# A transposition through DRAM with runs of 512 bytes, whole-piece column scales, and one piece turned on TensorE

## The chip, the cores and the metric

The kernel runs on one core of one Trainium2 chip. The metric is the device time of one execution in microseconds, the median of three runs. Names of engines: PE is TensorE, DVE VectorE, ACT ScalarE, POOL GpSimd, SP the queue engine that issues most transfers.

## The reference

Two layers of a trunk on a sequence of 256 positions and a model width of 2048, all float32. One layer in short:

```python
h = rmsnorm(x, g_pre)
u = h @ w_in                       # latents, B's q k v z, C's q k v z, A's z, gate logits
o_a = latent attention             # q and k normalised and scaled by column gains
o_b = differential attention       # bq = rope(rmsnorm(b_q, b_g_q)), bk likewise, heads of 2 x 64
o_c = chunked band attention       # cq = rmsnorm(c_q, c_g_q), ck likewise, heads of 128
branches = (o_a * silu(a_z), o_b * silu(b_z), o_c * silu(c_z))
y = sum(gates[n] * (branches[n] @ w_branch[n]) for n in range(3))
x = x + y @ w_out
```

Every product with a weight matrix contracts over the feature axis, so whatever was computed with positions on the partitions (q, k, the gated branch outputs, y, and x for the next layer) has to be transposed before it is multiplied again.

## The kernel before

The 256 positions are two row tiles of 128. All weights are streamed from DRAM once, in units of 512 output columns (`matunit`, L138 to L166). A unit walks over its rows in chunks of 256: SP issues the DMA of a chunk of 512 KB (tile `..._r`, L153, four buffers), ACT rounds it to the matmul format (`..._h`, L154, three buffers), DVE subtracts to get the rest (`..._l`, L155, three buffers), and PE does 12 matmuls of 128x512 with them: data hi times weight hi (L163), times weight lo (L164), and data lo times weight hi (L165). A unit over 2048 rows has 8 such chunks.

In the B and C halves (`b0`, `b1`, `c0`, `c1`, four heads each) the units come in the order k, q, v, z, and then the scores (L311 and L317). k and q are normalised with positions on the partitions (`qk_natural`), then transposed by `bounce`, and `from_bounced` splits the transposed piece to hi and lo with the column gain applied as a scale of ACT's and DVE's operation: L174 and L175 for C, L186 and L187 for B's q (`split_stacked`, four operations of 64x512 on each engine), L195 and L196 for B's k (`split_twice`, eight on each).

`bounce` (L218) transposes a piece of 256x512 in this way: DVE turns blocks of 32x32 in place (L223, two operations), one DMA writes the piece to DRAM in runs of 2 KB (L225), and four DMAs read it back, one for each 32 partitions, in runs of 32 floats = 128 bytes (L229, a source of 32 x 32 x 32). All five go by SP's queue, in order with the weight chunks. There are 42 such pieces over both layers: the latent (2), k and q of B and C (16), gated outputs of A and C (8) and of B (4), y (8) and x for layer 1 (4). On PE the same can be done by `to_transposed` (L202): eight transposes of 128x128 into PSUM, from where ACT and DVE split to hi and lo; so far branch A uses it.

At a layer's end `gate_branch(2)` makes the last of y, four pieces of 512 columns (`n2j0` to `n2j3`; product `l1n2j3b_p`, gate and sum on DVE at L655 and L657 into `yacc`). Each piece is bounced (`l1n2j3yz`) and split (`l1n2j3y`, L171 and L172). The output projection (`l1o_p`) contracts over y: its first unit needs y0 to y3 in turn.

The order on each engine is set at build time by the tile framework's scheduler, from a timing model of its own. An engine works its instructions off strictly in that order.

## Time and profile before

| | us |
|---|---|
| median of 3 runs (lowest, highest) | 2031.13 (2028.79, 2031.28) |
| the profiled execution | 2029.23 |
| its span, first to last instruction | 2027.3 |

All durations below come from the profiled execution. PE is busy for 1985.4 us of the span, DVE for 1267.4, ACT for 1107.0; the clock that PE was granted is at its full level in nearly all of the 40 slices of the page. Of 293,325 DMA packets 187,328 are under 512 bytes. In a timeline, a row gives the start, the duration, the engine and the line, what is written from what, how many like it are drawn together (x2), and in square brackets how long the engine had been idle before and who released it. "SPq" is the issue of a transfer, not the transfer.

### The profile page before, as it was taken

The numbers are of one execution on the slowest core, as the hardware profiler recorded it, in microseconds if no ns is written. First come the engines' busy times: TensorE is split into PE (matmuls) and PEld (weight loads), VectorE is DVE, ScalarE is ACT, GpSimd is POOL, SyncE is SP. The second block draws the span as 40 slices with busy tenths as digits, with TensorE's granted clock in tenths as the row PEclk, the third lists the DMA queues.
The fourth block names the chain that finished last, engine by engine and source line by source line (L and its number), as shares of the span: only waits on it lengthen the run. The fifth ranks groups of instructions, "written<-read, shape, count | busy, mean of one in ns | idle before, by whom it ended". The sixth has DMA issues, their size and how long they took to land.

```text
span 2027.3 us, 25409 instructions
## 1 busy us (share of the span) xinstructions
PE 1985.4 (98%) x9112; PEld 1647.3 (81%) x9112; DVE 1267.4 (63%) x1750; ACT 1107.0 (55%) x1624; POOL 225.4 (11%) x357
## 2 busy tenths in 40 slices
PE   9999999999999999998999999999999999999989
PEld 7888778888888888887888887788888888888867
DVE  5778777545666555555657777775456665555544
ACT  6677667545555544443556766664456564444433
POOL 2313040001000000000023220400010100000000
PEclk9999999999999999999999999999999999999989
DMA  8765565666776656677886665756676676657774
GB/s 295 219 188 175 186 207 187 207 204 209 223 210 212 192 191 197 215 235 241 260 237 205 180 181 173 227 178 209 204 220 214 203 217 189 196 197 211 235 228 156
DMA packets 293325, 421.39 MB, mean 208 GB/s; under 512 B 187328, under 2 KB 191424, under 8 KB 292432
## 3 DMA queue, kind: packets, MB, share of 16 engines
q1 hardware_dynamic: 290992, 410.80, 65.4%
q0 software_dynamic: 1920, 8.46, 1.3%
q8 instruction: 71, 1.16, 0.2%
q14 instruction: 54, 0.44, 0.1%
q10 hardware_dynamic: 288, 0.52, 0.1%
HBM read 393.51 MB, written 26.21 MB: 207 GB/s over the span
## 4 chain that ended last, share of the span: by engine, by line
PE 77%; DMA 8%; ACT 4%; POOL 3%; DVE 3%; issue 3%; SPq 2%; ACTq 0%; POOLq 0%; DVEq 0%
PE l1g_p L164 4%; PE l1g_p L165 4%; PE l1g_p L163 4%; PE l0g_p L164 4%; PE l0g_p L165 4%; PE l0g_p L163 4%; SPq L229 2%; PE l1o_p L163 1%; PE l1o_p L165 1%; PE l1o_p L164 1%; PE l0o_p L164 1%; PE l0o_p L163 1%; PE l0o_p L165 1%; DMA l0cq_r<-w 1%; PE l1az_p L164 1%
## 5 line engine op out<-in xcount | busy, mean ns | idle before, releaser
L155 DVE TENSOR_TENSOR l1g_l<-l1g_r,l1g_h 128x1024 fp32r<-128x1024 f32 x96 | 117.3, 1222 | 94.4 <-ACT l1g_h L154 94.3
L155 DVE TENSOR_TENSOR l0g_l<-l0g_r,l0g_h 128x1024 fp32r<-128x1024 f32 x96 | 117.2, 1222 | 93.3 <-ACT l0g_h L154 93.2
L154 ACT CAST l0g_h<-l0g_r 128x1024 fp32r<-128x1024 f32 x96 | 101.1, 1053 | 130.0 <-PE l0g_p L165 79.8
L154 ACT CAST l1g_h<-l1g_r 128x1024 fp32r<-128x1024 f32 x96 | 101.1, 1054 | 127.8 <-PE l1g_p L165 78.1
L164 PE MATMUL l0g_p<-l0g_l,xh 128*128 128x512 f32 x384 | 149.8, 390 | 0.0
L165 PE MATMUL l0g_p<-l0g_h,xl 128*128 128x512 f32 x384 | 149.7, 390 | 0.0
L164 PE MATMUL l1g_p<-l1g_l,xh 128*128 128x512 f32 x384 | 149.7, 390 | 0.0
L165 PE MATMUL l1g_p<-l1g_h,xl 128*128 128x512 f32 x384 | 149.7, 390 | 0.0
L163 PE MATMUL l1g_p<-l1g_h,xh 128*128 128x512 f32 x384 | 136.0, 389 | 0.0
L163 PE MATMUL l0g_p<-l0g_h,xh 128*128 128x512 f32 x384 | 136.0, 390 | 0.0
L164 PEld LDWEIGHTS l0g_p<-l0g_l,xh 128*128 128x128 f32 x384 | 72.1, 188 | 15.3 <-DVE l0g_l L155 0.5
L164 PEld LDWEIGHTS l1g_p<-l1g_l,xh 128*128 128x128 f32 x384 | 72.1, 188 | 14.8
L165 PEld LDWEIGHTS l1g_p<-l1g_h,xl 128*128 128x128 f32 x384 | 72.1, 188 | 14.7
L165 PEld LDWEIGHTS l0g_p<-l0g_h,xl 128*128 128x128 f32 x384 | 72.1, 188 | 14.7
L163 PEld LDWEIGHTS l0g_p<-l0g_h,xh 128*128 128x128 f32 x384 | 72.1, 188 | 14.7
L163 PEld LDWEIGHTS l1g_p<-l1g_h,xh 128*128 128x128 f32 x384 | 72.0, 188 | 14.7
L155 DVE TENSOR_TENSOR l1o_l<-l1o_r,l1o_h 128x1024 fp32r<-128x1024 f32 x32 | 39.2, 1224 | 46.1 <-ACT l1o_h L154 46.1
L154 ACT CAST l1o_h<-l1o_r 128x1024 fp32r<-128x1024 f32 x32 | 33.7, 1054 | 58.5 <-PE l1o_p L165 45.6
L155 DVE TENSOR_TENSOR l0o_l<-l0o_r,l0o_h 128x1024 fp32r<-128x1024 f32 x32 | 38.8, 1219 | 29.5 <-ACT l0o_h L154 29.5
L154 ACT CAST l0o_h<-l0o_r 128x1024 fp32r<-128x1024 f32 x32 | 33.3, 1051 | 39.5 <-PE l0o_p L165 32.0
L703 POOL DMA_DIRECT2D xres<-x x1 | 0.8, 784 | 309.5 <-DVE l0n2j3yz L223 309.5
L703 POOL DMA_DIRECT2D xres<-xscr x1 | 0.8, 792 | 308.8 <-DVE l1n2j3yz L223 308.8
(1600 smaller groups left out, 5866.3 us busy)
## 6 DMA issues: line engine op xcount, KB each, us to landing
l0g_r<-w SPq DMA_DIRECT2D x96, 512.0 KB, 3.6
l1g_r<-w SPq DMA_DIRECT2D x96, 512.0 KB, 4.2
l0o_r<-w SPq DMA_DIRECT2D x32, 512.0 KB, 4.9
l1o_r<-w SPq DMA_DIRECT2D x32, 512.0 KB, 4.4
l0az_r<-w SPq DMA_DIRECT2D x16, 512.0 KB, 4.7
l1az_r<-w SPq DMA_DIRECT2D x16, 512.0 KB, 4.7
l0b0k_r<-w SPq DMA_DIRECT2D x8, 512.0 KB, 3.7
l0b0q_r<-w SPq DMA_DIRECT2D x8, 512.0 KB, 3.3
```

Source lines behind the costliest of these rows:

```text
L154: state["cast"] = nc.scalar.copy(wh[:, ks, :N], wr[:, ks, :N])
L155: nc.vector.tensor_tensor(out=wl[:, ks, :N], in0=wr[:, ks, :N], in1=wh[:, ks, :N].bitcast(F32), op=ALU.subtract)
L163: nc.tensor.matmul(ps[t][:, :N], h[:, ts], wh[:, k2, :N], start=first, stop=False)
L164: nc.tensor.matmul(ps[t][:, :N], h[:, ts], wl[:, k2, :N], start=False, stop=False)
L165: nc.tensor.matmul(ps[t][:, :N], lo[:, ts], wh[:, k2, :N], start=False, stop=last)
L229: nc.sync.dma_start(flat[32 * j:32 * j + 32].rearrange("p (b i c) -> p b i c", b=HH, c=32), sv[j])
L703: nc.gpsimd.dma_start(xres, x_src.rearrange("(t p) d -> p t d", p=P))
```

## The change

`bounce` no longer turns in place. The DVE transposes write to a tile of their own (`..._tu`, from the pool of the z tiles), with the 32-wide blocks in another sequence, so that in DRAM the four blocks that one partition reads back lie side by side: each of the four reads is now 32 x 8 x 128 floats, in runs of 512 bytes instead of 128, 256 runs instead of 1024. In SBUF the piece then stands with the four 128-column blocks interleaved in steps of 32 columns (`bounced` and `as_bounced` are views of that), so the operations that split it read and write in runs of 32 elements.

The gain is applied first, by one ACT operation of 128x1024 in place over the whole piece (`from_bounced`, L251 in the changed file), and the split follows as plain copies and subtractions over the whole piece: `split_twice` has 4 + 4 operations of 64x1024 instead of 8 + 8 of 64x512, `split_stacked` 2 + 2 instead of 4 + 4. There are 20 such gain operations (16 for k and q of B and C, 4 for B's gated output). The latent and x keep the gain inside the split, block by block.

The last piece of y in each layer (`j = 3`) is not bounced; `to_transposed` turns it on PE (transposes at L204 in the changed file). 40 pieces go through DRAM instead of 42.

```diff
-    def split_twice(d0, d1, l0, l1, src, gain):
+    def split_twice(d0, d1, l0, l1, src):
         a, b = slice(0, 64), slice(64, P)
         for hi, lo, d, dl in ((a, b, d0, l0), (b, a, d1, l1)):
             for o in (hi, lo):
-                nc.scalar.activation(d[o], src[hi], AF.Copy, scale=gain[hi])
-                nc.vector.scalar_tensor_tensor(out=dl[o], in0=src[hi], scalar=gain[hi],
-                                               in1=d[hi].bitcast(F32), op0=ALU.mult, op1=ALU.subtract)
+                nc.scalar.copy(d[o], src[hi])
+                nc.vector.tensor_tensor(out=dl[o], in0=src[hi], in1=d[hi].bitcast(F32), op=ALU.subtract)
...
     def bounce(src, name, dst=None):
+        turned = zp.tile([P, NT, 4, HH, 32], F32, tag="z", name=f"{name}_tu")
+        scr = dram.tile([NT, P, 4, 128], F32, name=f"{name}_scr")
+        for t in range(NT):
+            nc.vector.transpose(turned[:, t].rearrange("p j b c -> p b j c"), src[:, t, :])
+        nc.sync.dma_start(scr.rearrange("t p j f -> p t (j f)"), turned.rearrange("p t j b c -> p t (j b c)"))
         dst = src if dst is None else dst
-        for t in range(NT):
-            nc.vector.transpose(dst[:, t, :], src[:, t, :])
-        scr = dram.tile([SEQ, 512], F32, name=f"{name}_scr")
-        nc.sync.dma_start(scr.rearrange("(t p) f -> p t f", p=P), dst)
-        sv = scr.rearrange("(i r) (b j c) -> j r b i c", r=32, b=HH, j=4, c=32)
         flat = dst.rearrange("p t f -> p (t f)")
+        sv = scr.rearrange("t (i r) j f -> j r (t i) f", r=32)
         for j in range(4):
-            nc.sync.dma_start(flat[32 * j:32 * j + 32].rearrange("p (b i c) -> p b i c", b=HH, c=32), sv[j])
-        return flat.rearrange("p (b q) -> p b q", b=HH)
+            nc.sync.dma_start(flat[32 * j:32 * j + 32].rearrange("p (q f) -> p q f", f=128), sv[j])
+        return flat
+    def bounced(z, b=None):
+        v = z.rearrange("p (q b c) -> p q b c", b=HH, c=32)
+        return v if b is None else v[:, :, b, :]
...
     def from_bounced(z, dh, dl, gain, per_block=False, put=None):
+        if per_block:
+            for b in range(HH):
+                split(as_bounced(dh[:, b, :]), as_bounced(dl[:, b, :]), bounced(z, b), gain(b))
+            return
+        if gain is not None:
+            nc.scalar.activation(z, z, AF.Copy, scale=gain)
         if put is not None:
-            for b0 in (0, 2):
-                put(slice(b0, b0 + 2), z[:, b0:b0 + 2, :])
-        elif per_block:
-            for b in range(HH):
-                split(dh[:, b, :], dl[:, b, :], z[:, b, :], gain(b))
+            put(bounced(z), as_bounced)
         else:
-            split(dh, dl, z, gain)
+            split(as_bounced(dh), as_bounced(dl), bounced(z))
...
         def b_split(z, hf, name, gain=None):
...
-            split(bh[hf], bl[hf], z, gain)
+            from_bounced(z, bh[hf], bl[hf], gain)
...
-                from_bounced(bounce(nat, f"{n}{nm}T"), None, None, None, put=put)
+                from_bounced(bounce(nat, f"{n}{nm}T"), None, None, cg[:, 1:2] if i == 0 else cg[:, 4:5], put=put)
...
                     yh[j], yl[j] = yt[:, 0], yt[:, 1]
-                    yz = zp.tile([P, NT, 512], F32, tag="z", name=f"{nm}yz")
-                    from_bounced(bounce(yacc[:, :, js], f"{nm}yT", yz), yh[j], yl[j], None)
+                    if j < 3:
+                        yz = zp.tile([P, NT, 512], F32, tag="z", name=f"{nm}yz")
+                        from_bounced(bounce(yacc[:, :, js], f"{nm}yT", yz), yh[j], yl[j], None)
+                    else:
+                        to_transposed(lambda t: yacc[:, t, js], 4, yh[j], yl[j], None, f"{nm}yT")
```

The last y piece on PE, end of layer 0. `yacc` holds y, `l0o_p` is the output projection's first unit, `l0o_h` and `l0o_l` its weights. Before, the projection's matmuls on y3 follow those on y2 directly:

```order
L163 MATMUL l0o_p_7847<-l0o_h_7939,l0n2j2y 128x512
L164 MATMUL l0o_p_7847<-l0o_l_7940,l0n2j2y 128x512
L165 MATMUL l0o_p_7847<-l0o_h_7939,l0n2j2y 128x512
L163 MATMUL l0o_p_7846<-l0o_h_7957,l0n2j3y 128x512
L164 MATMUL l0o_p_7846<-l0o_l_7958,l0n2j3y 128x512
L163 MATMUL l0o_p_7847<-l0o_h_7957,l0n2j3y 128x512
```

Now the transposes stand among the matmuls of the projection, 26 matmuls behind the last one of the branch product, and the first matmul on y3 comes 46 rows behind the transposes:

```order
L165 MATMUL l0o_p_7854<-l0o_h_7874,l0n2j0y 128x512
L163 MATMUL l0o_p_7853<-l0o_h_7892,l0n2j1y 128x512
L163 MATMUL l0o_p_7854<-l0o_h_7892,l0n2j1y 128x512
L204 MATMUL l0n2j3yT_t_7835<-ident,yacc_3440 128x128
L204 MATMUL l0n2j3yT_t_7842<-ident,yacc_3440 128x128
L204 MATMUL l0n2j3yT_t_7835<-ident,yacc_3440 128x128 x3
L204 MATMUL l0n2j3yT_t_7842<-ident,yacc_3440 128x128 x3
L164 MATMUL l0o_p_7853<-l0o_l_7893,l0n2j1y 128x512
```

So PE has the turning of y3 in its own order, with work on y1 and y2 between it and the first use of the result.

ACT in half b0 of layer 0, around the split of q; `l0b0z_h` are weight casts, `l0a_low` and `l0a_pp` belong to branch A's attention. Before:

```order
L154 CAST l0b0z_h_2138<-l0b0z_r_2137 128x1024
L154 CAST l0b0z_h_2156<-l0b0z_r_2155 128x1024
L186 ACTIVATE l0b0q<-l0b0q_n,cgain 64x512 x2
L374 COPY l0a_low<-l0a_o 128x128
L171 CAST l0a_pp<-l0a_pt 128x384
L174 ACTIVATE l0b0v_v<-l0b0v_p_1984,rcol_326 128x512
L174 ACTIVATE l0b0v_v<-l0b0v_p_1985,rcol_326 128x512
L186 ACTIVATE l0b0q<-l0b0q_n,cgain 64x512 x2
L154 CAST l0b0z_h_2174<-l0b0z_r_2173 128x1024
```

Now:

```order
L154 CAST l0b0z_h_2151<-l0b0z_r_2150 128x1024
L388 COPY l0a_low<-l0a_o 128x128
L171 CAST l0a_pp<-l0a_pt 128x384
L154 CAST l0b0z_h_2169<-l0b0z_r_2168 128x1024
L251 ACTIVATE l0b0q_n<-l0b0q_n,cgain 128x1024
L183 CAST l0b0q<-l0b0q_n 64x8x4x32 x2
L174 ACTIVATE l0b0v_v<-l0b0v_p_1979,rcol_326 128x512
L174 ACTIVATE l0b0v_v<-l0b0v_p_1980,rcol_326 128x512
L154 CAST l0b0z_h_2187<-l0b0z_r_2186 128x1024
L388 COPY l0a_low<-l0a_o 128x128
```

The third cast of the z weights moved from behind the split of q to ahead of it.

ACT in half b1 of layer 0, around the split of k; `l0b1v_h` are the casts of the v unit's eight chunks. Before, six of them stand ahead of the split of k (the last two are shown) and two behind it:

```order
L154 CAST l0b1v_h_2990<-l0b1v_r_2989 128x1024
L154 CAST l0b1v_h_3008<-l0b1v_r_3007 128x1024
L195 ACTIVATE l0b1k_2696<-l0b1k_n,cgain 64x512 x4
L195 ACTIVATE l0b1k_2697<-l0b1k_n,cgain 64x512 x4
L154 CAST l0b1v_h_3026<-l0b1v_r_3025 128x1024
L154 CAST l0b1v_h_3044<-l0b1v_r_3043 128x1024
L154 CAST l0b1z_h_3069<-l0b1z_r_3068 128x1024
L186 ACTIVATE l0b1q<-l0b1q_n,cgain 64x512 x2
```

Now five stand ahead, and the sixth stands behind the gain and the four copies of k:

```order
L154 CAST l0b1v_h_2978<-l0b1v_r_2977 128x1024
L251 ACTIVATE l0b1k_n<-l0b1k_n,cgain 128x1024
L195 CAST l0b1k_2692<-l0b1k_n 64x8x4x32 x2
L195 CAST l0b1k_2693<-l0b1k_n 64x8x4x32 x2
L154 CAST l0b1v_h_2996<-l0b1v_r_2995 128x1024
L154 CAST l0b1v_h_3014<-l0b1v_r_3013 128x1024
L154 CAST l0b1v_h_3032<-l0b1v_r_3031 128x1024
L251 ACTIVATE l0b1q_n<-l0b1q_n,cgain 128x1024
L154 CAST l0b1z_h_3057<-l0b1z_r_3056 128x1024
```

The eight scaled operations became one gain and four copies, and one more weight cast has to wait for them; the gain of q (L251) also came ahead of the first cast of the z unit.

## Rows read from the trace of the kernel before

**Rows 1.** Page, part 1: busy us, share of the span, instructions.

```profile
PE 1985.4 (98%) x9112; PEld 1647.3 (81%) x9112; DVE 1267.4 (63%) x1750; ACT 1107.0 (55%) x1624; POOL 225.4 (11%) x357
```

**Rows 2.** PE's waits: line waited for, us in total, times, longest us.

```profile
PE l1o_p L163 <- ACT l1n2j3y L171: 8.0, 1, 8.0
PE l0o_p L163 <- ACT l0n2j3y L171: 6.1, 1, 6.1
PE l0b1v_p L163 <- ACT l0b1v_h L154: 2.4, 1, 2.4
PE l0c_s L311 <- ACT l0c1q L174: 1.6, 1, 1.6
PE l0b0z_p L163 <- ACT l0b0z_h L154: 1.6, 1, 1.6
PE l1b0z_p L163 <- ACT l1b0z_h L154: 1.5, 1, 1.5
PE l0b1z_p L163 <- ACT l0b1z_h L154: 1.2, 1, 1.2
PE l1b1z_p L163 <- ACT l1b1z_h L154: 1.2, 1, 1.2
```

**Rows 3.** PE timeline at both layer ends: start us, us, instruction, idle before it.

```profile
942.28 0.80 PE L163 MATMUL l0o_p<-l0o_h,l0n2j3y 128*128 128x512 f32 x1 [6.07 <-ACT l0n2j3y L171]
947.14 0.39 PE L165 MATMUL l0o_p<-l0o_h,l0n2j3y 128*128 128x512 f32 x1
...
1949.88 0.79 PE L163 MATMUL l1o_p<-l1o_h,l1n2j3y 128*128 128x512 f32 x1 [8.02 <-ACT l1n2j3y L171]
1954.20 0.39 PE L164 MATMUL l1o_p<-l1o_l,l1n2j3y 128*128 128x512 f32 x1
```

**Rows 4.** Timeline of PE, DVE and SP, end of layer 1.

```profile
1925.15 0.39 PE L165 MATMUL l1n2j3b_p<-l1n2j3b_h,l1cbT1l 128*128 128x512 f32 x1
...
1926.29 1.28 DVE L657 TENSOR_TENSOR yacc<-yacc,l1n2j3g 128x512 f32<-128x512 f32 x2
...
1938.45 6.05 SPq L229 DMA_DIRECT2D l1n2j3yz<-l1n2j3yT_scr  x4
```

**Rows 5.** PE timeline, eight transposes of the a branch.

```profile
109.46 1.04 PE L205 MATMUL l0a0kT_t<-ident,l0a0k_n 128*128 128x128 f32 x8
```

**Rows 6.** ACT timeline, half b0, layer 0.

```profile
207.76 1.34 ACT L186 ACTIVATE l0b0q<-l0b0q_n,cgain 64x512 fp32r<-64x512 f32 x2 [5.02 <-DMA l0b0q_n<-l0b0qT_scr]
...
212.20 2.94 ACT L154 CAST l0b0z_h<-l0b0z_r 128x1024 fp32r<-128x1024 f32 x3
```

**Rows 7.** Windows: busy us of each engine, PEclk, DMA share, GB/s.

```profile
300.00:305.00 5.00, 3.84 (x10) 2.71 (x11) 4.60 (x5) 1.84 (x2) 0.00 (x0) 0.70 0.44 99
...
1220.00:1225.00 5.00, 4.48 (x11) 3.51 (x12) 4.97 (x8) 2.51 (x4) 0.00 (x0) 0.52 0.31 97
```

**Rows 8.** Timeline of SP, ACT, PE, half b1, layer 0.

```profile
288.52 3.53 SPq L229 DMA_DIRECT2D l0b1k_n<-l0b1kT_scr  x4
...
295.93 2.94 ACT L195 ACTIVATE l0b1k<-l0b1k_n,cgain 64x512 fp32r<-64x512 f32 x4 [0.33 <-DMA l0b1k_n<-l0b1kT_scr]
...
294.75 0.61 PE L163 MATMUL l0b1v_p<-l0b1v_h,xh 128*128 128x512 f32 x2
```

**Rows 9.** The same of half b1, layer 1.

```profile
1296.07 3.16 SPq L229 DMA_DIRECT2D l1b1k_n<-l1b1kT_scr  x4
...
1300.91 5.93 ACT L195 ACTIVATE l1b1k<-l1b1k_n,cgain 64x512 fp32r<-64x512 f32 x8 [0.94 <-DMA l1b1k_n<-l1b1kT_scr]
...
1307.96 0.73 PE L163 MATMUL l1b1v_p<-l1b1v_h,xh 128*128 128x512 f32 x2 [0.92 <-ACT l1b1v_h L154]
```

**Rows 10.** ACT timeline, half c1, layer 0.

```profile
629.33 1.15 ACT L174 ACTIVATE l0c1q<-l0c1q_n,cgain 128x1024 fp32r<-128x1024 f32 x1 [5.16 <-DMA l0c1q_n<-l0c1qT_scr]
```

**Rows 11.** Page, part 5: VectorE's lo of a chunk; busy us, mean ns.

```profile
L155 DVE TENSOR_TENSOR l1g_l<-l1g_r,l1g_h 128x1024 fp32r<-128x1024 f32 x96 | 117.3, 1222 | 94.4 <-ACT l1g_h L154 94.3
```

**Rows 12.** Page, part 6: a weight chunk's DMA, KB, us to landing.

```profile
l0b0k_r<-w SPq DMA_DIRECT2D x8, 512.0 KB, 3.7
```

More of the change, by code (lines that the diff above doesn't have):

```diff
@@ new lines, in as_bounced @@
+    def as_bounced(d):
+        if len(d.shape) == 2:
+            return d.rearrange("p (q c) -> p q c", c=32)
+        return d.rearrange("p b (q c) -> p q b c", c=32)
+    def from_bounced(z, dh, dl, gain, per_block=False, put=None):
+        if per_block:
[4 more added lines that the diff above has]
+            nc.scalar.activation(z, z, AF.Copy, scale=gain)
+        if put is not None:
+            put(bounced(z), as_bounced)
@@ L394, in simple_half @@
             o = attend_transposed(p, v, hl, n)
-            nc.vector.tensor_tensor(out=zt[:, hl, :], in0=o[:, :SEQ], in1=zt[:, hl, :], op=ALU.mult)
+            zc = bounced(zt, hl)
+            nc.vector.tensor_tensor(out=zc, in0=as_bounced(o[:, :SEQ]), in1=zc, op=ALU.mult)
         return zt
@@ L621, in trunk_kernel @@
                     d = [att_tile(f"{n}{nm}{m}") for m in range(2)]
-                    put = lambda bs, pt: split_twice(d[0][:, 0, bs, :], d[1][:, 0, bs, :], d[0][:, 1, bs, :],
-                                                     d[1][:, 1, bs, :], pt, cg[:, 4:5])
+                    put = lambda pt, v: split_twice(v(d[0][:, 0]), v(d[1][:, 0]), v(d[0][:, 1]), v(d[1][:, 1]), pt)
                 else:
@@ L626, in trunk_kernel @@
                     d = [d[:, 0], d[:, 1]]
-                    put = lambda bs, pt: split_stacked(d[0][:, bs, :], d[1][:, bs, :], pt, cg[:, 1:2])
-                from_bounced(bounce(nat, f"{n}{nm}T"), None, None, None, put=put)
+                    put = lambda pt, v: split_stacked(v(d[0]), v(d[1]), pt)
+                from_bounced(bounce(nat, f"{n}{nm}T"), None, None, cg[:, 1:2] if i == 0 else cg[:, 4:5], put=put)
                 op[nm] = d
```

## Prediction

> **What bounds the kernel now.** I read the page's busy shares first: PE is busy for 98% of the span [rows 1], so only PE's own idle time, its slow stretches and work added to it can move the end. What another engine or a queue saves counts only where PE waits for it. The list of PE's waits came second [rows 2]: the reader is to see that two waits, one per layer, are far longer than all others, both of the output projection for the split of y3, and that the next ones are weight casts (L154) in the halves b0 and b1 and the scores of c1, all in stages where a bounce is under way. Third, PE's timeline at the two layer ends [rows 3]: behind the long wait the matmuls run at half their rate for a while. Fourth, the order on ACT and PE, shown with the change.
>
> **y3 on PE.** The two waits, 8.0 and 6.1 us [rows 2], go if the transposes come in time. The slow matmuls behind them go too: in layer 0 eleven matmuls from 942.28 to 947.14 take 4.86 us where 11 x 0.23 = 2.5 is the normal rate, and in layer 1 ten take 4.32 instead of 2.3 [rows 3], so 2.4 and 2.0 us. That is 18.5 us in all. In time: y3 is summed by 1926.29 + 1.28 = 1927.6 in layer 1, the last branch matmul starts at 1925.15 [rows 4], and 26 matmuls later, at 1925.4 + 26 x 0.23 = 1931.4, PE reaches the transposes: 3.8 us of slack. The split from PSUM is about a cast and a lo of 1024 columns, 1.0 (three casts in 2.94 [rows 6]) plus 1.2 [rows 11]; the 46 matmuls ahead of y3's first use last 10.6 us and hide it. Before, the reads of y3 alone were issued 10.9 us after its sum was ready (1938.45 against 1927.6 [rows 4]). The price: eight transposes of 128x128 take 1.04 us from first start to last end [rows 5], so 16 add at most 2.1 us. Together -18.5 + 2.1 = **-16.4**. If they came one by one with the pipeline empty in between, 16 x 0.3 (twice the 0.13 of that row and more) would still be under 5.
>
> The Trainium skill ("TensorE: Matmul & The Clock Gate", Part 4: PE-mode transpose) gives some 275 to 390 ns for one such transpose; by it the price would be 4.4 to 6.2 us and the part -14.1 to -12.3. The row of this kernel, 1.04 us for eight, decides for the lower price.
>
> **Halves b0.** The wait of 1.6 us in layer 0 and 1.5 in layer 1 [rows 2] is for the third z cast. It starts at 212.20, since ACT had waited 5.02 us for the read of q, and then had the rest of q's split ahead of it [rows 6]. In the changed order that cast stands before the gain. What becomes late next is the fourth cast, behind gain, two copies and the v split (some 1.2 + 2.1 + 1.3 us): from the same landing at 207.8 that ends at 213.4. The third cast was there at 213.2 [rows 6] and PE had wanted it 1.6 us sooner; it wants the fourth a chunk, 2.7 us, later, at 214.3. So the waits go. In layer 1 the clock fell as well: 0.52 over 1220 to 1225 [rows 7], 5 x 0.48 = 2.4 us. Sum -1.6 - 1.5 - 2.4 = **-5.5**; it is nothing if another stall drops the clock in the same place, and not below that by the rows.
>
> **Halves b1, the part that speaks against the change.** One more weight cast, the sixth of v, now stands behind the split of k. Layer 0: the reads are issued at 288.52, and ACT is released by the last of them at 295.93 [rows 8], so four reads took 7.4 us; in layer 1 from 1296.07 to 1300.91 they took 4.8 [rows 9]. Four reads of the changed form move the same 512 KB as one weight chunk, which lands 3.7 us after its issue [rows 12]; I take 4.2 with the issues, and keep 7.4 and 4.8 as the other end. Then k has landed at 292.7, the gain (1.15 [rows 10]) ends at 293.9, four copies of 1.0 [rows 6] at 297.9, the sixth cast at 298.9. PE starts the sixth chunk at 294.75 [rows 8]: a wait of 4.1 us. Its lo stands on DVE behind the last lo of k (until 299.1) and ends at 300.3, another 0.95 after the two hi matmuls. So 5.1 us of waits stand against the 2.4 + 1.2 of before [rows 2], +1.5, and the clock loses 2.2 as at the layer ends instead of the 0.30 x 5 = 1.5 us of before [rows 7], +0.7: +2.2. Layer 1: landing at 1300.3, cast ready at 1306.4, lo at 1307.8; PE waited for the seventh cast from 1307.0 on [rows 9], so it wants the sixth at 1307.0 - 2.7 = 1304.3. Waits of 2.1 + 0.9 against 0.9 + 1.2: +0.9, and I add the clock loss of 1.5, which this stage did not have before: +2.4. Behind the waiting ACT operations stand casts 6 to 8 of v and the first of z, all due later by one chunk time each; they follow at 1.0 against PE's 2.7. Sum **+4.6**. Bounds: -7.2 if both stages run through (3.6 + 1.5 + 2.1 go); +8.4 if the reads land as before (+3.2 in layer 0, +0.6 in layer 1).
>
> **Halves c.** q needs gain and copy now, 1.15 + 1.0 instead of 1.15 [rows 10], and its gain stands ahead of the first z cast. Reads that land 0.6 to 3.2 us sooner, as in b1, pay for that in about half of the stages or more: **0**. Bounds: four stages with at most 1.6 each [rows 2] to gain, -6.4; or the extra operation in each with unshortened reads, 4 x 1.15 = +4.6.
>
> **Edits at nothing.** Strided output of the DVE transposes, and of the split's operations in runs of 32, fewer lo operations, a quarter of the read packets, shorter issues on SP: DVE is at 63% and ACT at 55% [rows 1], and outside the stages above PE never waits for them for long. Should strided operations take twice as long, the four copies of k alone would add 4 us in each b1 half.
>
> **Sum.** -16.4 - 5.5 + 4.6 + 0 = -17.3. Against the profiled execution, 2029.2 us, that is 2011.9. The median of the runs shown is 1.9 us above that execution, so **2014**.
>
> **Rivals.** *Everything lands early.* If writes, too, land sooner because the queues carry fewer packets, k comes in time and the waits of b1 and c vanish: -16.4 - 5.5 - 7.2 - 6.4 = -35.5, **1995**. For it: four reads in short runs took 4.8 to 7.4 us [rows 8, 9] for the bytes that a weight chunk lands in 3.7 [rows 12], so the run length counts. Against it: in layer 0, from the issue of the reads at 288.5 to PE's need at 294.75 there are 6.2 us, and gain, copies and cast alone are 6.15.
>
> The Trainium skill ("DMA: Bandwidth & Descriptors", Specifications) asks for 512 bytes and more per transfer for the line rate; the rows of the reads against that of the weights agree in kind, and by the rule this rival gains weight.
>
> *Landing is mostly a fixed delay.* Then the reads take what they took; b1 gets +8.4, c +4.6: -16.4 - 5.5 + 8.4 + 4.6 = -8.9, **2022**. For it: in layer 1 the four reads landed 4.8 us after the first issue, hardly above my 4.2. The same page (Anatomy of one DMA) puts most of some 2 us of a transfer into the receipt of the last write, which run length would not shorten; it says so of the GpSimd path, and no run here shows it apart.
>
> *The gain blocks ACT.* Twenty gain operations stand in ACT's order and wait for all four reads, ahead of weight casts that have only three buffers of lead. If each costs PE 1 us net, the 20 us outweigh the rest: 2029.2 - 21.9 + 20 + 4.6 + 1.9 = **2034**, slower. It decides from 17.3 / 20 = 0.87 us each. For it: ACT did stand still 5 us for a read in b0 and c1 [rows 6, 10]. Against it: in c those 5 us cost PE 1.6.
>
> **How the numbers follow.** Forecast 0.54 (2006 to 2021), early landing 0.13 (1992 to 2003), fixed delay 0.21 (2018 to 2027), gain blocks 0.12 (2027 to 2040). Leaving out about a tenth at either end gives 1999 to 2028. About 0.2%, 4 us, is what a measurement of this kernel can tell: faster 0.87, same 0.06 (the seam of the last two cases), slower 0.07.
>
> **What would show it.** PE's waits without the two o_p rows, sixteen transposes at L204 with no idle before them, the clock at full level at both layer ends (step one). No wait for l0b0z_h (step two). A wait of l0b1v_p of about 4 us at the sixth chunk, behind L195 (step three; if it is gone, the first rival, if it is 7, the second). ACT waits at L251 with casts late behind them in all stages would show the third. I am wrong if the y3 transposes wait for yacc, or if the waits that go at the layer ends come back in the projection's next chunks.

## The result, and the profile after

The changed kernel takes 2056.06 us in the median (2045.93 to 2057.24), the one before in the same runs 2029.96 (2025.32 to 2031.28): a ratio of 1.0122, with a 95% interval of 1.0085 to 1.0158. It is slower. Forecast were 2014 us and a range that ends at 2028; the sign was wrong. The profiled execution took 2055.62 us, its span 2053.9, that is 26.6 more than before. Part 1 of its page, against [rows 1]:

```profile
PE 2001.1 (97%) x9128; PEld 1653.3 (80%) x9128; DVE 1258.6 (61%) x1724; ACT 1127.3 (55%) x1632; POOL 225.1 (11%) x357
```

TensorE still bounds the kernel. It has 16 instructions more, the transposes, and is busy for 15.7 us more; its mean granted clock fell from 0.993 to 0.989. So of the 26.6 us 10.9 are waits (span without busy time, 41.9 us before and 52.8 now). Of the 15.7 the lower clock explains at most some 8 (0.7% of the span lost before, 1.1% now) and the transposes 2.1; some 6 are not taken apart here. Its waits after, against [rows 2] (line waited for, us in total, times, longest):

```profile
PE l1b1v_p L164 <- DVE l1b1v_l L155: 4.5, 2, 4.2
PE l0b1v_p L163 <- ACT l0b1v_h L154: 3.8, 1, 3.8
PE l0o_p L163 <- ACT l0o_h L154: 3.0, 2, 2.4
PE l1b1v_p L163 <- ACT l1b1v_h L154: 2.5, 1, 2.5
PE l0b1v_p L164 <- DVE l0b1v_l L155: 2.4, 1, 2.4
PE l0c_pt L352 <- DVE l0c1z L410: 2.4, 1, 2.4
PE l1c_pt L352 <- DVE l1c1z L410: 2.0, 1, 2.0
PE l1c0z_p L163 <- ACT l1c0z_h L154: 1.8, 1, 1.8
PE l0c1z_p L163 <- ACT l0c1z_h L154: 1.8, 1, 1.8
PE l0c_pt L352 <- DVE l0c0z L410: 1.8, 1, 1.8
```

The two long waits for y3 are gone, and so is that for the z casts of b0. What has come is small and everywhere: weight casts (L154) in b1, c0, c1 and the output projection, VectorE's rest of a weight chunk (L155), and in the C halves the gated output (L410). By the starts of the units on TensorE in both traces (one profiled execution each, as for all figures by stage below), the span divides like this, in us:

| stage | forecast | measured, layer 0 and 1 |
|---|---|---|
| layer end with y3 | -16.4 | -1.1 and -9.2 |
| b0 | -5.5 | +2.9 and -1.9 |
| b1 | +4.6 | +4.1 and +6.8 |
| C halves | 0 | +10.5 and +10.7 |
| start, and the gates where y0 to y2 are made | 0 | -1.0, and +1.7 and +3.0 |

They add up to +26.5, and 21.2 of it lie in the C halves, where the forecast had nothing.

What a C stage does now, on ACT and then on PE, half c1 of layer 0; [rows 10] is the same place before (in a timeline the columns are start, duration, engine and line, operation, and in brackets the idle time before it and its releaser):

```profile
638.42 1.15 ACT L251 ACTIVATE l0c1q_n<-l0c1q_n,cgain 128x1024 f32<-128x1024 f32 x1 [6.72 <-DMA l0c1q_n<-l0c1qT_scr]
639.48 1.03 ACT L154 CAST l0c1z_h<-l0c1z_r 128x1024 fp32r<-128x1024 f32 x1
```

```profile
640.56 0.73 PE L163 MATMUL l0c1z_p<-l0c1z_h,xh 128*128 128x512 f32 x2 [1.79 <-ACT l0c1z_h L154]
```

ACT stands still for 6.72 us with the gain at the head of its row. The first z cast behind it has nothing to do with q, but an engine takes its instructions in order, and so TensorE waits 1.79 us for a weight chunk that had landed at 630.9. Then it runs slowly for a while (windows: busy us of PE, PEld, DVE, ACT and POOL, granted clock, DMA share, GB/s):

```profile
640.00:645.00 5.00, 4.22 (x12) 3.10 (x13) 4.46 (x5) 4.49 (x6) 0.00 (x0) 0.68 0.36 104
680.00:685.00 5.00, 3.25 (x12) 2.66 (x13) 3.78 (x7) 1.53 (x2) 0.00 (x0) 0.78 0.38 129
300.00:305.00 5.00, 1.22 (x2) 0.50 (x2) 4.23 (x4) 3.38 (x4) 0.58 (x2) 0.55 0.49 170
305.00:310.00 5.00, 4.79 (x11) 3.81 (x12) 2.42 (x3) 0.84 (x1) 0.00 (x0) 0.50 0.87 212
```

A granted clock of 0.50 is the lower of two levels, 1.2 GHz; the 0.68 is a mean of it and of the full 2.4 GHz. In the first window twelve matmuls keep TensorE busy for 4.22 us, where twelve at 0.23, their pace at the full clock, take 2.7: some 1.5 us are lost, nearly as much as the wait itself. (The last two windows are those of b1, for later.) The second window holds the 2.4 us wait for c1's L410, the gate. Where that comes from is seen on ACT some 15 us earlier (L312 is the silu of z, L344 an exponential of the scores):

```profile
666.47 0.69 ACT L312 ACTIVATE l0c1z<-l0c1z_p,rcol 128x512 f32<-128x512 f32 x1 [0.31 <-PE l0c1z_p L165]
667.17 1.28 ACT L344 ACT_TABLE_LOAD   x1
...
668.94 1.28 ACT L312 ACT_TABLE_LOAD   x1
670.24 0.69 ACT L312 ACTIVATE l0c1z<-l0c1z_p,rcol 128x512 f32<-128x512 f32 x1
```

The new order puts an exponential between the two silus of z, in all four C halves. That costs two loads of a function table of 1.28 us each, and the second half of z, which has to go through DRAM whole before it can be gated, starts 3.8 us after the first (0.6 before). There are 40 such loads in this trace and 30 in that of before. All four C halves wait for the gate now, 7.7 us in all; the waits for z casts are 5.1 us, in three of them.

The x pieces in layer 0 show a wait of the first kind, without any separate gain (L174 is the split with its scale inside, as before):

```profile
998.92 1.71 ACT L174 ACTIVATE xh<-x1n,colt 128x256 fp32r<-128x256 f32 x4 [6.79 <-DMA x1n<-x1T_scr]
```

The split stands in ACT's row ahead of the seventh and eighth weight cast of the projection's unit; before it stood behind the seventh. TensorE waits 2.41 us for `l0o_h` there. With its other waits, this layer end gives back most of what y3 brought.

### The profile page after: what moved, and what is told of

It is laid out like the page before. It is cut to its first block, busy times and chain, and to the rows that moved or that the text cites. A ratio compares the mean times of both kernels' runs of the same rounds, so it can differ in the third digit from the quotient of the medians.

```text
span 2053.9 us, 25420 instructions
## 1 busy us (share of the span) xinstructions
PE 2001.1 (97%) x9128; PEld 1653.3 (80%) x9128; DVE 1258.6 (61%) x1724; ACT 1127.3 (55%) x1632; POOL 225.1 (11%) x357
## 2 busy tenths in 40 slices
DMA packets 161581, 419.29 MB, mean 204 GB/s; under 512 B 15136, under 2 KB 60192, under 8 KB 160688
## 4 chain that ended last, share of the span: by engine, by line
PE 66%; DMA 12%; ACT 6%; DVE 5%; issue 5%; POOL 4%; SPq 2%; ACTq 0%; DVEq 0%; POOLq 0%
PE l0g_p L164 4%; PE l0g_p L165 4%; PE l0g_p L163 4%; PE l1g_p L164 3%; PE l1g_p L165 3%; PE l1g_p L163 3%; SPq L230 2%; PE l1o_p L165 1%; PE l1o_p L163 1%; PE l1o_p L164 1%; DMA x1n<-x1T_scr 1%; PE l0o_p L164 1%; PE l0o_p L165 1%; PE l0o_p L163 1%; DMA x1T_scr<-x1T_tu 1%
## 5 line engine op out<-in xcount | busy, mean ns | idle before, releaser
L155 DVE TENSOR_TENSOR l0g_l<-l0g_r,l0g_h 128x1024 fp32r<-128x1024 f32 x96 | 116.8, 1222 | 89.4 <-ACT l0g_h L154 89.4
L155 DVE TENSOR_TENSOR l1g_l<-l1g_r,l1g_h 128x1024 fp32r<-128x1024 f32 x96 | 116.8, 1222 | 87.7 <-ACT l1g_h L154 82.8
L154 ACT CAST l0g_h<-l0g_r 128x1024 fp32r<-128x1024 f32 x96 | 100.6, 1053 | 124.3 <-PE l0g_p L165 68.0
L154 ACT CAST l1g_h<-l1g_r 128x1024 fp32r<-128x1024 f32 x96 | 100.7, 1053 | 122.6 <-PE l1g_p L165 64.6
L164 PEld LDWEIGHTS l0g_p<-l0g_l,xh 128*128 128x128 f32 x384 | 72.5, 189 | 17.3 <-DVE l0g_l L155 2.5
L155 DVE TENSOR_TENSOR l1o_l<-l1o_r,l1o_h 128x1024 fp32r<-128x1024 f32 x32 | 39.2, 1225 | 41.7 <-ACT l1o_h L154 41.7
L154 ACT CAST l1o_h<-l1o_r 128x1024 fp32r<-128x1024 f32 x32 | 33.7, 1055 | 53.2 <-PE l1o_p L165 48.2
L155 DVE TENSOR_TENSOR l0o_l<-l0o_r,l0o_h 128x1024 fp32r<-128x1024 f32 x32 | 38.6, 1220 | 28.1 <-ACT l0o_h L154 28.1
L154 ACT CAST l0o_h<-l0o_r 128x1024 fp32r<-128x1024 f32 x32 | 33.2, 1051 | 36.9 <-PE l0o_p L165 29.6
```

Of the source, the lines that this page charges most:

```text
L154: state["cast"] = nc.scalar.copy(wh[:, ks, :N], wr[:, ks, :N])
L155: nc.vector.tensor_tensor(out=wl[:, ks, :N], in0=wr[:, ks, :N], in1=wh[:, ks, :N].bitcast(F32), op=ALU.subtract)
L164: nc.tensor.matmul(ps[t][:, :N], h[:, ts], wl[:, k2, :N], start=False, stop=False)
```

## The experiments

Two theories stood at the start. **Order**: the order that is fixed at build time has the splits one weight chunk earlier, since it counts on reads in long runs landing sooner than they do; TensorE loses the time behind ACT's standing still. **Gain**: the twenty separate gain operations cost it, by their time and by their waits. All ratios are to the kernel before in the same runs. The medians come from several sets of runs, in which the kernel before takes 2029.3 to 2031.1 us; small differences are safer in the ratios.

**e1, only y3 on TensorE, everything else as before.**

```diff
+                    if j < 3:
                         yz = zp.tile([P, NT, 512], F32, tag="z", name=f"{nm}yz")
                         from_bounced(bounce(yacc[:, :, js], f"{nm}yT", yz), yh[j], yl[j], None)
+                    else:
+                        to_transposed(lambda t: yacc[:, t, js], 4, yh[j], yl[j], None, f"{nm}yT")
```

> Only the third piece of the change: the last y piece of each layer is transposed on TensorE, everything else is as before. Both theories below leave this part alone: the two waits of the output projection (8.0 and 6.1 us) and the slow matmuls behind them (4.4 us) go, sixteen transposes add at most 2.1 us, so 16 us less than before, about 2014 us (2010 to 2018). If the gain at the end of layer 0 is given back, as in the changed kernel, where that layer end won only 1 us, it is 8 to 10 us less, about 2021 us.

Measured: 2015.72 us, ratio 0.9937 (0.9914 to 0.9961). The span is 13.8 us shorter, with 7.3 and 9.2 at the two layer ends. This part is worth nearly what was forecast, where nothing else is changed.

**e2, the changed kernel with the round trip of before** (runs of 128 bytes, transposed in place), so with gain, y3 and the splits over whole pieces.

```diff
-        turned = zp.tile([P, NT, 4, HH, 32], F32, tag="z", name=f"{name}_tu")
-        scr = dram.tile([NT, P, 4, 128], F32, name=f"{name}_scr")
...
+            nc.vector.transpose(dst[:, t, :], src[:, t, :])
+        scr = dram.tile([SEQ, 512], F32, name=f"{name}_scr")
```

> The changed kernel with the DRAM round trip of before: reads in runs of 128 bytes, blocks turned in place, layout not interleaved; the gain operation over the whole piece and y3 on TensorE stay. Theory A (the order: with runs of 512 bytes the order made at build time puts the splits, and the gates on VectorE, one weight chunk earlier than the data lands, and weight casts stand behind them): with short runs the order has the casts ahead again, c and the x pieces cost nothing, b1 a few us, so 2010 to 2024 us. Theory B (the gain operation: 1.15 us more in twenty chains that wait for a read): the twenty operations are still there, so within 8 us of the changed kernel, 2046 to 2060 us.

Measured: 2032.26 us, ratio 1.002 (1.0007 to 1.0033). It hits neither: 16.5 us above e1, 24 below the changed kernel. So the gain costs something without the long runs, and the rest comes only with them. Between the profiled executions of e1 and e2, 18 of 21.6 us lie in the C halves, although q's gain stands behind the first z cast there, as q's split did before. What is new is the exponential between the silus. On ACT in e2, then in e3 (the next run), half c1 of layer 0:

```profile
659.08 0.69 ACT L309 ACTIVATE l0c1z<-l0c1z_p,rcol 128x512 f32<-128x512 f32 x1
...
662.96 0.69 ACT L309 ACTIVATE l0c1z<-l0c1z_p,rcol 128x512 f32<-128x512 f32 x1
```

```profile
659.63 1.27 ACT L310 ACTIVATE l0c1z<-l0c1z_p,rcol 128x512 f32<-128x512 f32 x2
```

**e3, the changed kernel without the twenty gains.**

```diff
-        if gain is not None:
-            nc.scalar.activation(z, z, AF.Copy, scale=gain)
```

> The changed kernel without the twenty gain operations: the column gains of B's and C's q and k and of B's gated output are left out of the computation, all copies and subtractions stay, reads in runs of 512 bytes and y3 on TensorE stay. Theory A (the order): the splits stand as early or earlier, weight casts still behind them, so 2040 to 2062 us. Theory B (the gain operation): what the change lost goes with it, 2012 to 2030 us.

Measured: 2031.19 us, ratio 1.0013 (0.9998 to 1.0028), just above what the gain theory allowed and below what the order theory did. Here are the long runs beside y3, with unscaled splits over whole pieces, and 15.5 us of e1's profit are gone. They do not lie in the C halves, which take what they took before (0.0 and -0.8 us). Between the profiled executions 12.5 us are lost against e1: 5.2 in the gates where y0 to y2 are made, 3.8 at the end of layer 0, 5.0 at the starts of the two layers, 2.5 in b1, 1.5 in C, and b0 gains 5.6. ACT's order fits that: the splits of y and x stand behind the seventh weight cast in e1 and behind the sixth in e3, that of k in b1 behind the sixth (e1) or seventh (e2) v cast and in e3 behind the fourth. Y3 alone leaves the order as it was (e1), so it is the round trip, or the merged splits without a scale, that moves it; no run has these splits with short runs and without gains.

That q's place alone is not what costs C shows here too. In all four C halves of e3 q's split stands ahead of the first z cast and ACT stands still for 4.1 to 5.4 us before it, yet TensorE waits for no z cast longer than 0.15 us. On ACT in c1 of layer 0:

```profile
631.90 1.05 ACT L171 CAST l0c1q<-l0c1q_n 128x1024 fp32r<-128x1024 f32 x1 [4.09 <-DMA l0c1q_n<-l0c1qT_scr]
632.86 1.99 ACT L154 CAST l0c1z_h<-l0c1z_r 128x1024 fp32r<-128x1024 f32 x2
```

**e4, the changed kernel with the splits back behind the casts that they stood behind before, in C and b1** (`behind` calls the split ahead of a chunk, and the framework's `issue_after` keeps it behind the chunk's last cast).

```diff
+        def behind(chunk, fn):
+            def pre(c):
+                if c == chunk:
+                    with tc.issue_after(state["cast"].ins):
+                        fn()
+            return pre
...
+            v = vsplit(in_unit(f"c{hf}v", 512, behind(1, late["k"])), rcol, f"{n}v")
+            zc[hf] = silu_gate(in_unit(f"c{hf}z", 512, behind(1, late["q"])), rcol, f"{n}z")
```

> The changed kernel with all its operations, but with the order of ScalarE as before at the places where it had changed: gain and split of k behind the first v cast in C and behind the sixth in b1, of q behind the first z cast in C and the third in b1, the split of the x pieces behind the fourth cast after them. Theory A (the order): the waits for z and o casts behind gain or split go (5 us in C, 4 at the end of layer 0, 6 to 9 in b1) with the slow matmuls behind them (about 8), and the waits of the C heads for the gate on VectorE stay (8 us with their slow matmuls), so 2026 to 2038 us. Theory B (the gain operation): the chains are as long as before, 2050 to 2058 us.

Measured: 2030.45 us, ratio 1.0004 (0.9989 to 1.0019). The C halves fall from +10.5 and +10.7 to -2.5 and -2.3 us against before, with all gains in place: there it was the order, and the silus of z stand together again (0.6 us apart). In b1 q stands behind the second z cast, not behind the third as expected. The x pieces still stand behind the sixth cast, as in the changed kernel, and the y pieces were left alone.

**e5, the same in all places**: y and x too stand behind the seventh cast again, k and q of b1 one chunk later than in e4 (so k stands one cast and q two casts later than in the kernel before).

```diff
+                pg = in_unit(f"g{n}{j}", 512, behind(7, y_late[0]) if y_late else None)
...
+                x_pre = behind(7, x_late)
```

> The changed kernel with the casts of the weights ahead everywhere: beside what the fourth run held back in C, the split of k in b1 now stands behind the seventh v cast and that of q behind the third z cast, the y pieces behind the seventh cast of the next gate unit, the x pieces behind the seventh cast of the next unit. In the fourth run 7 us more than in the first were left at the end of layer 0 (o casts behind the x splits), 5 in the gate units of branch c (casts behind the y splits) and some 3 in b1. If the order is what costs (theory A), these go: 2010 to 2020 us, no slower than the first run (2016) by more than 4. If the longer chains of gain and copy cost in any order (theory B), it stays at 2026 to 2032.

Measured: 2017.07 us, ratio 0.9941 (0.9924 to 0.9957). The operations and transfers are those of the changed kernel; the order alone, on ACT and what the build then does with the other engines, is worth 39 us (37 by the ratios). The same q in c1 of layer 0, on ACT:

```profile
627.46 1.15 ACT L259 ACTIVATE l0c1q_n<-l0c1q_n,cgain 128x1024 f32<-128x1024 f32 x1 [2.10 <-DMA l0c1q_n<-l0c1qT_scr]
628.52 1.03 ACT L155 CAST l0c1z_h<-l0c1z_r 128x1024 fp32r<-128x1024 f32 x1
```

(A weight cast is at L155 in the kernels with `behind`, VectorE's rest at L156.) ACT stands still 2.10 us instead of 6.72, and TensorE does not wait for the cast.

**e6, e5 without the gains.** The edit is that of e3.

> The fifth kernel without the twenty gain operations (the column gains of B's and C's q and k and of B's gated output are left out of the computation). Theory A: with the casts ahead the gain costs next to nothing, so within 4 us of the fifth run. Theory B: each gain in a chain costs 0.5 to 1 us, so 10 us or more below the fifth run.

Measured: 1997.54 us, ratio 0.9842 (0.9827 to 0.9858), 20 us below e5. All of it lies in the B halves (in b0 3.0 and 4.7 us, in b1 5.8 and 8.1); the C halves are the same with and without, within 0.5 us. So with the splits held back the gain is a cause of its own only in B; why there, this run does not show.

**e7, the changed kernel with y3 through DRAM.**

```diff
-                    if j < 3:
+                    if True:
```

> The changed kernel with the last y piece of each layer sent through DRAM again, like the other three. If y3 on TensorE is worth in the changed kernel what it was worth in the first run, 14 us, this is 2070 us (2066 to 2074). If the shorter reads had already taken a part of the two waits, or the order at the end of layer 0 differs, it is less: 2058 to 2066.

Measured: 2061.79 us, ratio 1.0159 (1.014 to 1.0178). Taking y3 back costs only some 6 us here, not 14, and by the two ratios, 1.0159 and 1.0122, with their intervals even that is not clear of noise. At the two layer ends of the profiled executions it is 4.4 and 6.9 us: the waits for y3 are 4.7 and 5.9 us long, where they were 6.1 and 8.0, so the shorter round trip had taken a part of them.

**e8, e5 with the gains of the B halves on VectorE.**

```diff
+                nc.vector.tensor_scalar(out=z, in0=z, scalar1=gain, scalar2=None, op0=ALU.mult)
```

> The fifth kernel with the gain of the B halves (q, k and the gated output) as one operation of VectorE over the whole piece instead of ScalarE; C's gains stay on ScalarE, all gains are applied. The sixth run was 20 us below the fifth, all of it in the B halves. If the gain costs because it takes ScalarE's time ahead of the copies and the weight casts behind them, it is free here: 1996 to 2004 us. If it costs because it lengthens the chain from the read to the last copy, VectorE's operation lengthens it about as much: 2012 to 2020 us.

Measured: 2017.07 us, ratio 0.9937 (0.9919 to 0.9954), as e5. The operation is shorter there (0.75 us for 1.15), but takes the standing still along. VectorE, half b1 of layer 0:

```profile
296.72 0.75 DVE L260 TENSOR_SCALAR l0b1k_n<-l0b1k_n,cgain 128x1024 f32<-128x1024 f32 x1 [4.75 <-DMA l0b1k_n<-l0b1kT_scr]
297.39 1.22 DVE L156 TENSOR_TENSOR l0b1v_l<-l0b1v_r,l0b1v_h 128x1024 fp32r<-128x1024 f32 x1
```

VectorE stands 4.75 us with a weight chunk's rest (L156) behind the gain, and TensorE waits for these rests instead of for casts:

```profile
PE l0b1v_p L165 <- DVE l0b1v_l L156: 4.5, 3, 2.4
PE l1b1v_p L165 <- DVE l1b1v_l L156: 2.7, 2, 2.4
```

**e9 and e10, the gain as the scale of the split again**, which leaves nothing out of the computation: as many ACT operations as without it, now scaled, and on VectorE four by blocks of 256 columns for one of 1024. e9 has it in e5, e10 in the changed kernel with its own order.

```diff
-        if gain is not None:
-            nc.scalar.activation(z, z, AF.Copy, scale=gain)
...
-                nc.scalar.copy(d[o], src[hi])
-                nc.vector.tensor_tensor(out=dl[o], in0=src[hi], in1=d[hi].bitcast(F32), op=ALU.subtract)
+                nc.scalar.activation(d[o], src[hi], AF.Copy, scale=gain[hi])
+                for b in range(HH):
+                    nc.vector.scalar_tensor_tensor(out=dl[o][:, :, b], in0=src[hi][:, :, b], scalar=gain[hi],
+                                                   in1=d[hi][:, :, b].bitcast(F32), op0=ALU.mult, op1=ALU.subtract)
```

> e5's order (all splits behind the casts where they stood before), 512-byte round trip, y3 on TensorE, and no separate gain: the column gain goes back into the splits as a scale, one ScalarE operation per piece as in e6, and on VectorE four operations by blocks of 256 columns instead of one of 1024 (16 for a k of B instead of 4). ScalarE's order is that of e6, nothing is left out. Theory A, the 20 us between e5 and e6 are the separate gain standing still in an in-order row: it is gone here too, 1996 to 2008 us. Theory B, whatever lengthens the way from the landing to the next weight chunk's lo costs, on either engine: sixteen operations of some 0.48 us (the scaled lo of 128x256) are 7.7 us instead of 4.9, so 2.8 us more than in e6, about what the gain took, and the waits for l0b1v_l and l1b1v_l come back with 2 to 4 us: 2010 to 2022 us.

> The changed kernel with the gain in the splits as in e9, and the build-time order left alone (ScalarE's order is then nearly that of e3, splits of k and q one or two weight chunks earlier than before). Nothing is left out. If the order is the larger cause: 2027 to 2042 us, near e3 or some us above it, waits of l0b1v_h and l1b1v_h of 2 us and more. If the separate gain is what counts: below 2020 us.

Measured: e9 2004.67 us, ratio 0.9867 (0.985 to 0.9884); e10 2046.47 us, ratio 1.0081 (1.0056 to 1.0106). e9 is the fastest kernel that computes everything, 26 us below the one before in the same runs and 11 below e1 (14 by the ratios). Theory A's range holds for e9, but B's wait came too. VectorE and then TensorE in e9, b1 of layer 0:

```profile
295.30 6.75 DVE L211 SCALAR_TENSOR_TENSOR l0b1k<-l0b1k_n,cgain,l0b1k 64x256 fp32r<-64x256 f32 x16
302.08 1.23 DVE L156 TENSOR_TENSOR l0b1v_l<-l0b1v_r,l0b1v_h 128x1024 fp32r<-128x1024 f32 x1
```

```profile
303.36 0.79 PE L165 MATMUL l0b1v_p<-l0b1v_l,xh 128*128 128x512 f32 x1 [2.44 <-DVE l0b1v_l L156]
```

The sixteen scaled rests take 6.75 us, four unscaled ones in e6 4.91, and TensorE waits 2.44 us for the chunk behind them (0.6 in e6). That explains a part of the 7 us between e9 and e6. e10 lies 4 us above its upper forecast; its waits (3.6 and 3.4 us for L155, 3.2 and 2.6 for L154 in the b1 halves) are of the kind foreseen.

Together six kernels with long runs and y3 on TensorE make a table, in us:

| | gain apart | gain in the split | no gain |
|---|---|---|---|
| order of the build | 2056.1 (after) | 2046.5 (e10) | 2031.2 (e3) |
| splits kept behind the casts | 2017.1 (e5) | 2004.7 (e9) | 1997.5 (e6) |

Down a column, the order is worth 34 to 42 us whatever is done with the gain. Along a row, the separate operation costs 10 or 12 us against the scale inside the split; by the ratios it is 8 and 15, and the 8 is not clear of noise (1.0122 +- 0.0036 against 1.0081 +- 0.0025). Left out altogether, the gain is worth 25 and 20 us. Nothing in the second row is slower than before.

That the columns come out alike hides that the time is lost in different places. The C halves of both layers together, against the kernel before:

| kernel | runs, gain, order | start of the first silu of z to that of the second | C halves |
|---|---|---|---|
| after | 512 bytes, apart, of the build | 3.8 us | +21.2 us |
| e7 | the same, y3 through DRAM | 3.8 | +15.2 |
| e2 | 128 bytes, apart, of the build | 3.9 | +15.8 |
| e10 | 512 bytes, in the split, of the build | 3.8 | +5.9 |
| e3 | 512 bytes, none, of the build | 0.6 | -0.8 |
| e4, e5 | 512 bytes, apart, splits held back | 0.6 | -4.8, -4.4 |

C loses time only in the kernels in which the build has put an exponential between the silus, and most where the gain is an operation of its own; the long runs alone lose it elsewhere (e3). No run moves the silus by themselves, so how the 21.2 us divide between gates and z casts is not shown beyond the waits above.

## Why the prediction was wrong

**The landing was sized well, its use was not.** The four reads of a piece were issued in 2.81 us instead of 3.53, and k of b1 in layer 0 was there 5.07 us after the first issue; before it took 7.4 [rows 8]. Over all pieces, first issue to last landing fell from 6.7 to 5.2 us in the median. SP and then ACT:

```profile
289.94 2.81 SPq L230 DMA_DIRECT2D l0b1k_n<-l0b1kT_scr  x4
```

```profile
295.01 1.15 ACT L251 ACTIVATE l0b1k_n<-l0b1k_n,cgain 128x1024 f32<-128x1024 f32 x1 [4.07 <-DMA l0b1k_n<-l0b1kT_scr]
296.20 4.24 ACT L195 CAST l0b1k<-l0b1k_n 64x1024 fp32r<-64x1024 f32 x4
300.46 2.94 ACT L154 CAST l0b1v_h<-l0b1v_r 128x1024 fp32r<-128x1024 f32 x3
```

I had assumed 4.2. The rivals on landing are both out as the main story: the writes take 4.3 us either way, so not everything lands early, and the reads did get shorter, so landing is not mostly a fixed delay. The Trainium skill asks for 512 bytes and more per transfer for the line rate ("DMA: Bandwidth & Descriptors", Specifications). These rows agree in kind; no run here measures the line rate.

Two landings of before were misread. The rows at 1300.91 [rows 9] and 207.76 [rows 6] are operations on 64 partitions, which the second of the four reads released; all four had landed only at 1302.9 (6.9 us after the first issue, not 4.8) and at 210.8. The gain runs over 128 partitions and waits for all four. With 6.9 the upper bound of b1 would have been +10.5 and not +8.4, the fixed delay 2024, and its best argument, 4.8 hardly above 4.2, was none.

**The failed step is "Halves c: 0", and with it "Edits at nothing".** Forecast (-17.3) and measurement (+26.5) lie 43.8 us apart: 21.2 are the C halves, some 6 each the layer ends, b0 and b1, and 3.7 the stages put at nothing. I read that q's gain had moved ahead of the first z cast, priced only the operation, 1.15 us, against the shorter landing, and did not read the rest of ACT's row. Measured are +21.2 us, far outside the bounds of -6.4 and +4.6. What the runs show in place of the 0: with the separate gain in its row, the build's order makes TensorE wait 5.1 us for z casts and 7.7 us for gates whose silus an exponential has parted, and it runs at the lower clock behind four of these waits (from 641.8, 682.8, 1566.8 and 1665.8), some 1.7 us lost each. Either half of the cause taken away takes the cost away: the order held back with all gains in place (e4, -4.8), or the gains left out in the build's own order (e3, -0.8). The bounds were built from waits and operations of the order before, and could not hold a cost that comes from the order itself. The x and y pieces, which I put among the edits at nothing since they have no gain, moved ahead of one cast each; that is where the long runs alone cost time (e3).

**y3 on TensorE was right where it stands alone.** Layer 1 gained 9.2 us, as worked out (8.0 + 2.0 less some 1). The sum of y3 is ready at 1962.00 + 1.28 = 1963.3; DVE, PE and ACT show:

```profile
1962.00 1.28 DVE L671 TENSOR_TENSOR yacc<-yacc,l1n2j3g 128x512 f32<-128x512 f32 x2
```

```profile
1966.99 1.04 PE L204 MATMUL l1n2j3yT_t<-ident,yacc 128*128 128x128 f32 x8
```

```profile
1967.74 1.07 ACT L171 CAST l1n2j3y<-l1n2j3yT_t 128x512 fp32r<-128x512 f32 x2
```

That is 3.7 us of slack where 3.8 were forecast, 1.04 us for the eight as in [rows 5], and no wait. In layer 0 the last sentence of the prediction came true: the waits came back in the projection's next chunks, behind the x splits, and -7.3 (e1) became -1.1.

**b0** lost the wait for the z casts (1.55 us became 0.17). But the scheduler had also put k's four copies in one go (4.24 us) ahead of a v cast, for which TensorE now waits 1.4 us, and the fourth z chunk's rest is 1.05 us late. That last wait was in the rows of before: from the landing of all four reads, 210.8, the fourth cast ends at 216.4 and not at 213.4, behind the 214.3 at which PE wants it. -5.5 became +1.0. On PE in layer 0:

```profile
186.34 0.73 PE L163 MATMUL l0b0v_p<-l0b0v_h,xh 128*128 128x512 f32 x2 [1.40 <-ACT l0b0v_h L154]
...
218.01 0.73 PE L163 MATMUL l0b0z_p<-l0b0z_h,xh 128*128 128x512 f32 x2 [0.17 <-ACT l0b0z_h L154]
219.79 0.50 PE L164 MATMUL l0b0z_p<-l0b0z_l,xh 128*128 128x512 f32 x1 [1.05 <-DVE l0b0z_l L155]
```

**b1** had the right sign and less than half the size, +4.6 for +10.9. In layer 0 the waits are 3.8 + 2.4 us instead of the 5.1 worked out, and the clock fell for longer, to 0.55 and 0.50 in the two windows from 300 to 310 shown above: thirteen matmuls keep TensorE busy for 6.0 us there instead of 3.0, so 3.0 us are lost instead of 2.2. In layer 1 I had let the weight's rest follow k's last rest at once; q's norm and transposes stand in between, and the weight's rest came 4.2 us late instead of 0.9. On VectorE:

```profile
1319.14 0.94 DVE L283 TENSOR_TENSOR l1b1q_n<-l1b1q_n,l1b1q_ss 128x512 f32<-128x512 f32 x1 [2.67 <-POOL l1b1q_ss L281]
1320.00 0.70 DVE L224 STREAM_TRANSPOSE l1b1qT_tu<-l1b1q_n 128x512 f32<-128x512 f32 x1
1320.63 2.44 DVE L196 TENSOR_TENSOR l1b1k<-l1b1k_n,l1b1k 64x1024 fp32r<-64x1024 f32 x2
1323.82 0.71 DVE L224 STREAM_TRANSPOSE l1b1qT_tu<-l1b1q_n 128x512 f32<-128x512 f32 x1 [0.76 <-POOL l1b1q_n L301]
1324.57 2.45 DVE L196 TENSOR_TENSOR l1b1k<-l1b1k_n,l1b1k 64x1024 fp32r<-64x1024 f32 x2
1327.05 3.50 DVE L155 TENSOR_TENSOR l1b1v_l<-l1b1v_r,l1b1v_h 128x1024 fp32r<-128x1024 f32 x3
```

**The rival "The gain blocks ACT"** had the right side and the right mechanism, a row that stands still with casts behind it, for 2034 us. It was nearer than its 0.12: left out of the changed kernel the gains give back 25 us, against its 20. It named the waiting row but not the order that the build makes around it, which counts for more: with that held back the gains cost 20 us and the kernel is still faster than before (e5), and the places move with the long runs even without any gain (e3).

**What stays open.** Singly, the gain costs 16.5 us over e1 (e2) and the long runs 15.5 (e3), together 40 (after): some 8 us appear only with both (5 by the ratios), which is within the noise of the four medians. No run has the splits over whole pieces without gain, long runs or held order. SP's row differs as well: in the b1 halves of e5 k's write stands a weight chunk later than in e6 and e9, so the 12 us between e5 and e9 are those of the gain and of what the build does with it. e8 has k's write and reads where e9 has them and is as slow as e5, which speaks for the gain's own place. A gain on POOL was not tried.

## What to carry to other kernels

When a transfer gets shorter in a scheduler's eyes, read the new order of each in-order engine before pricing the transfer: every operation that waits for the landing and has moved ahead of the main stream's work can cost what its engine then stands still for, less the lead that the main stream has, at each place where the pattern repeats (in c1 6.72 us cost a wait of 1.79 with the gain, and 4.09 cost nothing without it). Read the order of the operations that were not changed as well: here two silus were parted. Ask of a wait which of several transfers it needs. Keep what depends on a late transfer behind the main stream's work by an explicit order, and put a scale into an operation that is there anyway instead of adding one in front. Try the parts of a change singly: here one was worth 14 us by itself, and the others hid it.

## What the runs showed of the hardware

A read in runs of 512 bytes cost SP 0.446 us of issue in the median against 0.672 for 128 bytes (40 and 42 pieces, four reads each), and landed in 3.2 us instead of 3.9 (medians); the write before it took 4.3 us either way, and so the round trip became shorter by less than the packets became fewer (161,581 instead of 293,325). Each of the eight transposes lasts 0.27 us in the trace and eight take 1.04, so in a row they start about every 0.11 us; the Trainium skill gives 275 to 390 ns for one of 128x128, measured in bf16 ("TensorE: Matmul & The Clock Gate", Part 4: PE-mode transpose). The single duration here, in f32, agrees with the lower figure; the price in a row, 1.04 / 8 = 0.13 us, is less than half of it. A gain over 128x1024 in place took 1.15 us on ScalarE and 0.75 on VectorE. Runs of 32 elements cost the engines nothing: k's copies of 64x1024 take 1.04 us interleaved (after) and 1.05 in blocks (e2), VectorE's subtractions 1.22 in both, and the transposes into another tile 0.71, as in place, so the strided layout is not what the change lost by. From the end of a silu to the start of an exponential behind it there were 1.31 us (667.16 to 668.47), hardly more than the 1.28 of the table load in between.
